# One change to a two-block transformer kernel: the low part of k in a tile of 128 rows per piece

## The chip, the cores and the metric

The kernel is one launch on one core of a Trainium2 chip. The metric is the device time of that launch in microseconds. TensorE multiplies matrices and writes to PSUM; in the profile its matmuls are PE and its loads of the stationary operand PEld. VectorE is DVE, ScalarE ACT, GpSimd POOL, and SyncE (SP) starts most transfers.

## The reference

One sequence of 1024 tokens with 1024 features goes through two layers of a first hybrid block and one layer of a second one. Each layer runs several branches on the normed input and mixes them. Two of the branches are softmax attention that reads the changed code:

- In each layer of the first block, a differential attention with a bias for each relative position. Each of 4 heads has two pieces m of q and k with 64 features; the two softmaxes are subtracted.
- In the second block, a causal attention whose logits get a decay, the difference of a running sum of log forget gates at the query and at the key. It has 4 heads of 64 features, and two heads lie in one projected block of 128 rows.

```python
logits = jnp.einsum('bqhmd,bkhmd->bhmqk', q_blk, k).astype(jnp.float32) * scale + bias
p = jax.nn.softmax(logits, axis=-1)
attn = p[:, :, 0] - lam * p[:, :, 1]
...
logits = jnp.einsum('bqhd,bkhd->bhqk', q[:, start:end], k[:, :end]) * scale
logits = logits + (f_q[..., :, None] - f_k[..., None, :])
```

Retention, pooling, a delta rule, a latent attention, a gated linear attention, gates and an MLP make up the rest; they are not touched.

## The kernel before

All products are in float32 accuracy from operands split in two parts: hi, the value rounded to the matmul's format, and lo, the rest. A product is hi x hi + hi x lo + lo x hi (`mm3`, lines L113 to L115), three matmuls into one PSUM bank. Most of the time goes into such dense products, with 128 rows of stationary operand and 256 or 512 columns.

**Logits of a piece.** A piece has 64 features, half of the array's 128 rows. `q_stack` puts hi and lo of a piece of q above each other in one page: rows [hi; lo] for m = 0 and [lo; hi] for m = 1. `k_stack` makes for each piece a page [hi; hi]. The first matmul (L386) then has 128 rows and gives q_hi k_hi + q_lo k_hi at once. What is missing is q_hi k_lo: `k_stack` keeps both pieces' lo parts in one page `kl`, that of m = 0 in rows 0 to 63 and that of m = 1 in rows 64 to 127, and the second matmul (L387) takes the 64 rows of its piece alone. Its stationary operand is the 64 rows of the q block that hold hi.

**First block, `attention_a`.** For each of 4 heads and 8 blocks of 128 queries, both pieces get logits of 1024 keys in two halves of 512: eight matmuls, L386 and L387 in turn. VectorE adds the bias and finds the maximum (L487), ScalarE takes the exponential (L491), VectorE inverts the sum (L492, L495), ScalarE scales the first piece (L496), VectorE subtracts the second (L497). Later TensorE transposes the result (L510), ScalarE and VectorE split it (L104, L105), and TensorE multiplies it with v. There are two banks for logits ("lg") and one for transposed blocks ("tp"). After each half of a head, a norm: sums on TensorE (L198), one small power on GpSimd (L141), and a broadcast of it on TensorE (L206).

**Second block, `fox`.** The same `k_stack`, `q_stack` and `qk_logits` feed `causal_heads`. Blocks reach only as far as the causal mask lets them, in parts of 512 or 256 keys. The last part of a block is followed by a matmul that adds the mask (L1461).

**What sets the order.** The projections of the next heads are put in a queue, and `pump` takes from it between the steps of attention. A scheduler then orders the instructions of each engine by priority when the kernel is built, and gives out pages. In the first block, all tiles of up to 512 columns come from 32 shared pages (tag "S"); a new tile waits until the last readers of the page's old tile are done. In the second block `q`, `kh` and `kl` have pages of their own.

Of the kernel before, what the change touches and what calls it, by code (L numbers as in the profile page):

```python
# [11 lines left out]
F32 = mybir.dt.float32  # L12
# [18 lines left out]
class Kern:  # L31
# [15 lines left out]
    # ---------------------------------------------------------------- tiles  # L47
# [4 lines left out]
    @contextmanager  # L52
    def phase(self, name):
        """A pool for the tiles of one phase; its bytes are waited for tile by tile."""
        old = self.pool
        with self.tc.tile_pool(name=self.nm(name), bufs=1, reuse_waits="tile") as self.pool:
            yield self.pool
        self.pool = old
# [38 lines left out]
    # ---------------------------------------------------------------- small helpers  # L97
# [19 lines left out]
    def log_sigmoid(self, out, x, n, tag):  # L117
        """out = log(sigmoid(x)) = min(x, 0) - log1p(exp(-|x|)), log1p(e) = 2 atanh(e / (2 + e))."""
        nc = self.nc
        if n <= 16:  # L120
            a, z, w = (self.small(n, tag + c, 2) for c in "azw")
        else:
            a, z, w = (self.T(tag + c, 1, F32, (P, n)) for c in "azw")
        nc.vector.scalar_tensor_tensor(out=a, in0=x, scalar=-1.0, in1=x, op0=ALU.mult, op1=ALU.max)
        nc.scalar.activation(a, a, AF.Exp, scale=-1.0)
        nc.vector.tensor_scalar_add(z, a, 2.0)
        nc.vector.reciprocal(z, z)
        nc.vector.tensor_tensor(out=z, in0=z, in1=a, op=ALU.mult)
        nc.vector.tensor_tensor(out=w, in0=z, in1=z, op=ALU.mult)
        nc.vector.tensor_scalar_mul(a, w, 1.0 / 13.0)  # L130
        for k in (11.0, 9.0, 7.0, 5.0, 3.0):
            nc.vector.scalar_tensor_tensor(out=a, in0=a, scalar=1.0 / k, in1=w, op0=ALU.add, op1=ALU.mult)
        nc.vector.scalar_tensor_tensor(out=a, in0=a, scalar=1.0, in1=z, op0=ALU.add, op1=ALU.mult)
        nc.vector.tensor_single_scalar(out=w, in_=x, scalar=0.0, op=ALU.min)
        nc.vector.scalar_tensor_tensor(out=out, in0=a, scalar=-2.0, in1=w, op0=ALU.mult, op1=ALU.add)

    def rsqrt_small(self, out, ss, n, mean):
        """out = (ss * mean + eps) ** -0.5 for a few columns."""
        nc = self.nc
        nc.vector.tensor_scalar(out=out, in0=ss, scalar1=mean, scalar2=EPS, op0=ALU.mult, op1=ALU.add)  # L140
        nc.gpsimd.tensor_tensor(out=out, in0=out, in1=self.mhalf[:, 0:n], op=ALU.pow)  # L141

    # ---------------------------------------------------------------- weights
    def wload(self, src, nk, n, hi=None, lo=None):
        """src: [128, nk, n] in DRAM -> accessors of the exact parts hi, lo of each k block."""
# [21 lines left out]
    def fm(self, out, w, X, half):  # L167
        """out[feature, token] += w^T X over all k blocks, for 512 tokens."""
        nk = len(w)
        for k in range(nk):  # L170
            xh, xl = X[k][half]
            self.mm3(out, w[k][0], w[k][1], xh, xl, k == 0, k == nk - 1)

    def tm(self, out, X, w, t):
        """out[token, feature] += X^T w for the 128 tokens of tile t."""
        nk = len(w)
        sl = slice((t % 4) * P, (t % 4 + 1) * P)
        for k in range(nk):
            xh, xl = X[k][t // 4]
            self.mm3(out, xh[:, sl], xl[:, sl], w[k][0], w[k][1], k == 0, k == nk - 1)  # L180

    # ---------------------------------------------------------------- norms
# [9 lines left out]
    def tok_sums(self, accs):  # L192
        """column sums of each [128, 512] page, token-major: [128, 4 per page] in PSUM."""
# [7 lines left out]
    def tok_bcast(self, r):  # L201
        """[128 tokens, n] -> [128, 128 n] in PSUM, the same in every partition."""
# [6 lines left out]
    def rnorm(self, acc, mean):  # L209
        """(mean * column sums of acc + eps) ** -0.5 in every partition, in PSUM."""  # L210
# [12 lines left out]
    # ---------------------------------------------------------------- set up  # L223
# [31 lines left out]
    def t5_table(self, rb, ohs):  # L255
        """bias of each relative position -1023..1023, each row shifted by one: skew[h][p][127 + j - p]."""
# [17 lines left out]
    # ---------------------------------------------------------------- first block  # L274
# [7 lines left out]
    def layer_consts(self, l, c, row, col):  # L282
# [21 lines left out]
        # retention decays; columns (direction, head)  # L304
# [30 lines left out]
    def silu_gate(self, ps, out):  # L335
        """out = (1 + tanh(x / 2)) * x = 2 silu(x), x in PSUM."""
# [4 lines left out]
    def q_stack(self, wq, X, half, nq=5):  # L341
        """Two 64-row pieces m of a 128-row block, scaled by 1/8: rows [hi; lo] (m = 0) or [lo; hi] (m = 1)."""
# [11 lines left out]
    def k_stack(self, wk, X, half, nk=5, nl=3):  # L354
        """Per piece rows [hi; hi], and lo at the rows where q has hi."""
# [4 lines left out]
        k0, k1, kl = self.T("kh", nk, F32R), self.T("kh", nk, F32R), self.T("kl", nl, F32R)  # L360
# [4 lines left out]
        nc.vector.tensor_tensor(out=kl[a], in0=pk[a], in1=k0[a].bitcast(F32), op=ALU.subtract)  # L365
        nc.vector.tensor_tensor(out=kl[b], in0=pk[b], in1=k1[b].bitcast(F32), op=ALU.subtract)  # L366
        return k0, k1, kl

    def qk_pack(self, qs, ks):
        return [[qs[0][m], qs[1][m]] for m in range(2)], [[ks[0][m], ks[1][m]] for m in range(2)], [ks[0][2], ks[1][2]]  # L370
# [8 lines left out]
    def qk_logits(self, out, QKK, m, qb, k0, kn, more=False):  # L379
        """out = q_m(block qb) . k_m(k0 : k0 + kn), all within one half."""  # L380
# [4 lines left out]
        rows = slice(m * 64, m * 64 + 64)  # L385
        mm(out, Q[m][qb // 4][:, sl], KH[m][half][:, o:o + kn], start=True, stop=False)  # L386
        mm(out, Q[m][qb // 4][rows, sl], KL[half][rows, o:o + kn], start=False, stop=not more)  # L387

    # -- the dense products of a layer, traced between the steps that wait for other engines
# [15 lines left out]
    def layer_dense(self, l, H, c, mixed, pre):  # L405
# [38 lines left out]
        # the first head: the work on the first half of the tokens goes ahead  # L444
# [20 lines left out]
    def attention_a(self, l, c, mixed):  # L465
        nc = self.nc
        tail = None
        for h in range(4):
# [6 lines left out]
            for qb in range(8):  # L475
# [4 lines left out]
                for m in range(2):  # L480
                    QKK = ({m: {half: qs[half][m]}}, {m: [ks[0][m], ks[1][m]]}, [ks[0][2], ks[1][2]])
# [57 lines left out]
    def diff_finish(self, h, half, osb, g, c, mixed):  # L539
        """in two steps; the first returns the second"""  # L540
# [234 lines left out]
    def out_proj(self, l, mixed, xold, xsave, sums, after):  # L775
        """x + mixed @ w_out, feature-major, one half of the tokens after the other."""
# [105 lines left out]
    def norm_next(self, half, xs, accs, wcol):  # L882
        """norm_half in steps"""
# [13 lines left out]
    def norm_between(self, half, xs, accs):  # L897
        """x2 = rmsnorm(x, final) -> DRAM; parts of rms_norm(x2, mix_pre).  mean(x2^2) = mean((x w)^2) r^2.  In steps."""
# [29 lines left out]
    # ---------------------------------------------------------------- second block  # L928
# [3 lines left out]
    def start_fills(self, H):  # L932
        """half 0 of the first units goes before half 1 of the tokens is there"""
# [6 lines left out]
    def fill(self, n=1):  # L940
        """The next n products of the gates, sigmoid(w_gate^T h + b) as 1 + tanh(./2), kept in DRAM until the branches are
        there: work for the tensor engine that nothing waits for."""
# [13 lines left out]
    def pre2(self, H):  # L956
        """the narrow projections: low-rank gate input (rows 0-15), b, a, f (rows 32-43), k_pe and its rotation (64-127)."""
# [83 lines left out]
    # ---- gated delta rule  # L1041
# [171 lines left out]
    def head_norm(self, t, o, gain, out):  # L1213
        """rms norm of each head's 64 columns of o: [128, 2, 2, 64] in PSUM, heads (b, m); out holds the gates.
        What waits for the norms is returned, to be traced later."""
# [21 lines left out]
    def delta_conv(self, b, j, H, cw):  # L1237
        """silu(causal convolution) of one 128-row block of q (j = 0), k, v; twice its value."""
# [99 lines left out]
    # ---- causal softmax attention, two heads of a block  # L1338
    def causal_heads(self, heads, steps):
        """Per head: start() -> logits(psum, qb, s, k0, kn, last), which adds q . k and the mask; V() -> [128, 4, 256] parts, columns vs;  # L1340
        out: [64 rows, 1024] feature-major pages.  A block's transposes follow the next block's logits."""
# [61 lines left out]
    def drain(self):  # L1403
        """traces what is left of the queue and forgets its results"""
        self.pump(len(self.dense))
        self.ready = {}
# [69 lines left out]
    def mla(self, H, out):  # L1476
# [4 lines left out]
        with self.phase("M") as mp:  # L1481
            # low-rank inputs, normed over their features
# [32 lines left out]
            def rope(ps, hs):  # L1515
                """rows 64-95 of ps rotated, at rows 64-95 of the result"""
# [86 lines left out]
    def gla_decays(self, g, up, gb):  # L1603
        """log decays, token-major [128, 4 of 8 tiles, 128 channels], kept in DRAM"""
# [12 lines left out]
    def gla(self, H, out):  # L1617
# [4 lines left out]
        with self.phase("G"):  # L1622
# [14 lines left out]
            # q, k, v  # L1637
# [108 lines left out]
    def merge(self, br):  # L1746
        """sum_i gate_i * (branch_i @ up_i), then @ w_out, feature-major; the last gates and the two halves of the tokens
        overlap."""
# [67 lines left out]
    def mlp(self, H, out):  # L1816
        """The first and the last part of the hidden layer take one half of the tokens after the other, so that the norms
        before and after have products beside them."""
# [42 lines left out]
        def finish(half, X):  # L1861
            """the last norm, in steps"""
# [116 lines left out]
def _lay(w, order):  # L1979
    """[K, N] -> [128, ...]: one run per partition for each group of columns, k blocks outermost."""  # L1980
# [67 lines left out]
def _cols(v):  # L2048
    """[..., n * 128] vectors -> [128, n] columns, one per block of 128."""
# [67 lines left out]
```

## Time and profile before

| | us |
|---|---|
| median of 3 runs | 3627.74 (3627.08 to 3628.82) |
| span of the profiled execution, first to last instruction | 3623.3 |
| what the median has beyond the span | 4.4 |
| TensorE matmuls busy | 3499.2 (97%) |
| VectorE, ScalarE, GpSimd busy | 1964.2, 1319.4, 89.6 |

The profiled execution's own time is not listed beside the runs; its span and the 4.4 us around it stand for it. The page counts the time from an instruction's start to its modelled end as busy. Matmuls are pipelined, so these times overlap: a matmul of 512 columns shows 0.39 us, but the next one may start 0.23 us after it. What TensorE really needs is read from starts. Idle time of the weight loader (PEld) is time in which no load ran; it costs something only where the matmul behind it is late.

### The profile page before, as it was taken

The page shows a single profiled execution, that of the slowest core. Times are in us where ns is not written, and L with a number is a line of the kernel's source. Part 1 is how long each engine was busy: PE and PEld are TensorE (multiplying, and loading weights), DVE is VectorE, ACT ScalarE, POOL GpSimd, SP SyncE. Part 2 cuts the span into 40 slices and gives each one's busy share as a digit, 9 for nine tenths or more (in the row PEclk, how much of TensorE's full clock was granted, in tenths as well). Part 3 has the DMA queues.
Part 4 walks back from the last instruction along what each step waited for, and adds up shares of the span by engine and source line. Part 5 has one row for each costly group of instructions (what it writes and reads, how often), then busy time and mean ns, then how long its engine had stood idle before and what let it go on. Part 6 is the DMA issues. An engine that isn't in the chain of part 4 may idle for free. (4 is left out here: it accounts for less than half of the span.)

```text
span 3623.3 us, 45361 instructions
## 1 busy us (share of the span) xinstructions
PE 3499.2 (97%) x18341; PEld 2835.2 (78%) x18341; DVE 1964.2 (54%) x3378; ACT 1319.4 (36%) x2098; POOL 89.6 (2%) x92
## 2 busy tenths in 40 slices
PE   7999999999999999999999999999999999999998
PEld 5777888777777788787777777877877778888886
DVE  6666654555666644556573466444268753333336
ACT  4555422233555422243322244454233442222222
POOL 0000000000000000000000000000000000000000
PEclk9999999999999999999999999999999999999999
DMA  5111111353110111354232211112156441111114
GB/s 182 47 40 41 42 48 51 112 183 110 49 41 30 31 33 57 108 161 153 74 119 62 81 47 57 47 53 87 53 191 227 143 126 49 53 47 47 53 55 149
DMA packets 138706, 302.34 MB, mean 83 GB/s; under 512 B 23944, under 2 KB 41336, under 8 KB 137984
## 3 DMA queue, kind: packets, MB, share of 16 engines
q1 hardware_dynamic: 129280, 282.65, 25.1%
q10 hardware_dynamic: 9216, 16.78, 1.2%
q8 instruction: 144, 2.36, 0.3%
q14 instruction: 66, 0.54, 0.0%
HBM read 245.30 MB, written 58.28 MB: 84 GB/s over the span
## 5 line engine op out<-in xcount | busy, mean ns | idle before, releaser
L113 PE MATMUL mm<-H,whi 128*128 128x512 f32 x2400 | 963.4, 402 | 28.1 <-DVE S L366 5.8
L115 PE MATMUL mm<-H,wlo 128*128 128x512 f32 x2400 | 952.0, 397 | 5.4 <-DVE wlo L105 5.4
L114 PE MATMUL mm<-H,whi 128*128 128x512 f32 x2400 | 951.7, 397 | 1.5 <-DVE H L105 1.5
L104 ACT CAST whi<-raw 128x1024 fp32r<-128x1024 f32 (+1 forms) x340 | 334.3, 984 | 857.0 <-PE mm L114 770.5
L105 DVE TENSOR_TENSOR wlo<-raw,whi 128x1024 fp32r<-128x1024 f32 (+1 forms) x340 | 387.4, 1141 | 440.5 <-ACT whi L104 427.8
L113 PEld LDWEIGHTS mm<-H,whi 128*128 128x128 f32 x2400 | 458.4, 191 | 133.5 <-issue 18.2
L115 PEld LDWEIGHTS mm<-H,wlo 128*128 128x128 f32 x2400 | 457.0, 190 | 103.5 <-DVE wlo L105 10.2
L114 PEld LDWEIGHTS mm<-H,whi 128*128 128x128 f32 x2400 | 457.3, 191 | 92.5 <-DVE H L105 2.6
L113 PE MATMUL mm<-whi,H 128*128 128x256 f32 x960 | 276.7, 289 | 3.5 <-DVE S L574 3.2
L114 PE MATMUL mm<-wlo,H 128*128 128x256 f32 x960 | 275.9, 288 | 1.4 <-DVE wlo L105 1.4
L115 PE MATMUL mm<-whi,H 128*128 128x256 f32 x960 | 274.4, 286 | 0.0
L113 PE MATMUL mm<-M,whi 128*128 128x512 f32 x640 | 249.8, 391 | 1.8 <-ACT whi L104 1.5
L115 PE MATMUL mm<-M,wlo 128*128 128x512 f32 x640 | 249.8, 391 | 0.2 <-DVE wlo L105 0.2
L114 PE MATMUL mm<-M,whi 128*128 128x512 f32 x640 | 249.8, 390 | 0.0
L113 PEld LDWEIGHTS mm<-whi,H 128*128 128x128 f32 x960 | 184.7, 193 | 8.6 <-issue 6.9
L114 PEld LDWEIGHTS mm<-wlo,H 128*128 128x128 f32 x960 | 184.8, 193 | 4.1 <-DVE wlo L105 2.0
L115 PEld LDWEIGHTS mm<-whi,H 128*128 128x128 f32 x960 | 184.8, 193 | 1.3 <-issue 1.2
L487 DVE CUSTOM_DVE_ANT_0 lg<-lg,strip 128x1024 f32<-128x1024 f32 x128 | 156.3, 1232 | 50.3 <-PE lg L387 49.6
L1853 DVE TENSOR_TENSOR Y<-Y,mm 128x512 f32<-128x512 f32 x112 | 77.0, 688 | 159.3 <-PE mm L115 159.2
L491 ACT ACTIVATE L<-lg,mx 128x1024 f32<-128x1024 f32 x128 | 142.5, 1119 | 29.0 <-DVE mx L487 15.6
L104 ACT CAST L<-tp 128x512 fp32r<-128x512 f32 x128 | 75.1, 586 | 207.1 <-PE tp L510 206.5
L113 PEld LDWEIGHTS mm<-M,whi 128*128 128x128 f32 x640 | 120.2, 188 | 28.1 <-ACT whi L104 2.0
(450 smaller groups left out, 5082.6 us busy)
## 6 DMA issues: line engine op xcount, KB each, us to landing
raw<-in_w_in SPq DMA_DIRECT2D x106, 512.0 KB, 3.7
raw<-in_w_out SPq DMA_DIRECT2D x48, 512.0 KB, 4.1
raw<-in_w_gate SPq DMA_DIRECT2D x46, 512.0 KB, 3.7
raw<-in_w_mlp_in SPq DMA_DIRECT2D x40, 512.0 KB, 3.6
raw<-in_w_mlp_out SPq DMA_DIRECT2D x40, 512.0 KB, 3.6
Y<-gates SPq DMA_DIRECT2D x64, 256.0 KB, 5.0
gates<-gs ACTq DMA_DIRECT2D x60, 256.0 KB, 2.0
mix<-S SPq DMA_DIRECT2D x48, 256.0 KB, 2.1
```

The source lines that it names most:

```text
L104: nc.scalar.copy(hi, src)
L105: nc.vector.tensor_tensor(out=lo, in0=src, in1=hi.bitcast(F32), op=ALU.subtract)
L113: mm(out, lh, rh, start=start, stop=False)
L114: mm(out, lh, rl, start=False, stop=False)
L115: mm(out, ll, rh, start=False, stop=stop)
L487: nc.vector.tensor_tensor_reduce(out=lg, in0=lg, in1=strip[:, w0:w0 + 1024], op0=ALU.add, op1=ALU.min, scale=-1.0, scalar=3.0e38, accum_ou ...
L491: nc.scalar.activation(pm, lg, AF.Exp, bias=mx, scale=-1.0, accum_out=sm)
L1853: nc.vector.tensor_tensor(out=Y[d][half], in0=Y[d][half], in1=pt, op=ALU.add)
```

## The change

`k_stack` gets two tiles for the lo parts instead of one. Tile `l0` holds the lo part of piece 0 in rows 0 to 63 and zeros in rows 64 to 127; `l1` holds zeros in rows 0 to 63 and the lo part of piece 1 in rows 64 to 127. The zeros are written by GpSimd, one memset for each tile at each call. The second matmul of the logits then takes all 128 rows of the q block, and its rows of q_lo meet zeros. Callers pass the tile of the piece. In the second block the tag `kl` has five pages instead of three. The rest of the diff takes out comments and docstrings.

```diff
-    def k_stack(self, wk, X, half, nk=5, nl=3):
-        """Per piece rows [hi; hi], and lo at the rows where q has hi."""
+    def k_stack(self, wk, X, half, nk=5, nl=5):
+
         nc = self.nc
         a, b = slice(0, 64), slice(64, 128)
         pk = self.ps("mm")
         self.fm(pk, wk, X, half)
-        k0, k1, kl = self.T("kh", nk, F32R), self.T("kh", nk, F32R), self.T("kl", nl, F32R)
+        k0, k1 = self.T("kh", nk, F32R), self.T("kh", nk, F32R)
+        l0, l1 = self.T("kl", nl, F32R), self.T("kl", nl, F32R)
+        nc.gpsimd.memset(l0[b].bitcast(F32), 0.0)
+        nc.gpsimd.memset(l1[a].bitcast(F32), 0.0)
         nc.scalar.copy(k0[a], pk[a])
         nc.scalar.copy(k0[b], pk[a])
         nc.scalar.copy(k1[b], pk[b])
         nc.scalar.copy(k1[a], pk[b])
-        nc.vector.tensor_tensor(out=kl[a], in0=pk[a], in1=k0[a].bitcast(F32), op=ALU.subtract)
-        nc.vector.tensor_tensor(out=kl[b], in0=pk[b], in1=k1[b].bitcast(F32), op=ALU.subtract)
-        return k0, k1, kl
+        nc.vector.tensor_tensor(out=l0[a], in0=pk[a], in1=k0[a].bitcast(F32), op=ALU.subtract)
+        nc.vector.tensor_tensor(out=l1[b], in0=pk[b], in1=k1[b].bitcast(F32), op=ALU.subtract)
+        return k0, k1, l0, l1
...
-        rows = slice(m * 64, m * 64 + 64)
         mm(out, Q[m][qb // 4][:, sl], KH[m][half][:, o:o + kn], start=True, stop=False)
-        mm(out, Q[m][qb // 4][rows, sl], KL[half][rows, o:o + kn], start=False, stop=not more)
+        mm(out, Q[m][qb // 4][:, sl], KL[m][half][:, o:o + kn], start=False, stop=not more)
...
-                    QKK = ({m: {half: qs[half][m]}}, {m: [ks[0][m], ks[1][m]]}, [ks[0][2], ks[1][2]])
+                    QKK = ({m: {half: qs[half][m]}}, {m: [ks[0][m], ks[1][m]]}, {m: [ks[0][2 + m], ks[1][2 + m]]})
```

The lines of the logits become L388 and L389 and most lines behind them move by two. The scheduler leaves nearly all instructions of TensorE, VectorE and ScalarE where they were. On TensorE, a block of logits of the second head stands so before (lg is the bank, S are pages: first k, then q):

```order
L510 MATMUL tp_1423<-c_ident,L_1263 128x128 x4
L386 MATMUL lg_1439<-S_1044,S_1226 128x512
L387 MATMUL lg_1439<-S_1046,S_1226 128x512
L386 MATMUL lg_1439<-S_1117,S_1226 128x512
L387 MATMUL lg_1439<-S_1119,S_1226 128x512
L386 MATMUL lg_1450<-S_1045,S_1227 128x512
L387 MATMUL lg_1450<-S_1046,S_1227 128x512
L386 MATMUL lg_1450<-S_1118,S_1227 128x512
L387 MATMUL lg_1450<-S_1119,S_1227 128x512
L510 MATMUL tp_1430<-c_ident,L_1263 128x128 x4
```

The same place on TensorE now:

```order
L512 MATMUL tp_1435<-c_ident,L_1275 128x128 x4
L388 MATMUL lg_1451<-S_1050,S_1238 128x512
L389 MATMUL lg_1451<-S_1052,S_1238 128x512
L388 MATMUL lg_1451<-S_1126,S_1238 128x512
L389 MATMUL lg_1451<-S_1128,S_1238 128x512
L388 MATMUL lg_1462<-S_1051,S_1239 128x512
L389 MATMUL lg_1462<-S_1053,S_1239 128x512
L388 MATMUL lg_1462<-S_1127,S_1239 128x512
L389 MATMUL lg_1462<-S_1129,S_1239 128x512
L512 MATMUL tp_1442<-c_ident,L_1275 128x128 x4
```

The places are the same. The two pieces read S_1046 both before; now piece 0 reads S_1052 and piece 1 S_1053.

GpSimd's queue from the norm of the first layer's input to the norms of the first and second head stands so before (rn is the small power of a norm):

```order
L141 TENSOR_TENSOR rn_336<-rn_336,mhalf 128x4
L141 TENSOR_TENSOR rn_1248<-rn_1248,mhalf 128x4
L141 TENSOR_TENSOR rn_1617<-rn_1617,mhalf 128x4
L141 TENSOR_TENSOR rn_1987<-rn_1987,mhalf 128x4
L141 TENSOR_TENSOR rn_2422<-rn_2422,mhalf 128x4
```

The same stretch of that queue now, up to the second of these norms of heads:

```order
L141 TENSOR_TENSOR rn_339<-rn_339,mhalf 128x4
L362 MEMSET S_659 64x512
L363 MEMSET S_660 64x512
L362 MEMSET S_1052 64x512
L363 MEMSET S_1053 64x512
L362 MEMSET S_1128 64x512
L363 MEMSET S_1129 64x512
L141 TENSOR_TENSOR rn_1260<-rn_1260,mhalf 128x4
L362 MEMSET S_1606 64x512
L363 MEMSET S_1607 64x512
L362 MEMSET S_1692 64x512
L363 MEMSET S_1693 64x512
```

Six memsets stand in front of the first head's first norm and four in front of its second; four more stand in front of the fifth norm of a layer, and the same again in the second layer. S_1606 and S_1607, for the third head, wait for the last logits that read the first head's k.

On ScalarE, between two blocks of the second head, the order before was (L104 with whi is the hi part of a weight load, L348 and L349 are q's copies, L104 with tp a split of transposed blocks):

```order
L496 ACTIVATE L_1263<-L_1263,smx_1264 128x1024
L348 ACTIVATE S_1306<-mm_1281 64x512
L349 ACTIVATE S_1307<-mm_1281 64x512
L104 CAST L_1166<-tp_1312 128x4x128
L104 CAST whi_1563<-raw_1561 128x1024
L104 CAST L_1167<-tp_1319 128x4x128
```

And at the same place on ScalarE now:

```order
L498 ACTIVATE L_1275<-L_1275,smx_1276 128x1024
L104 CAST whi_1575<-raw_1573 128x1024
L104 CAST L_1178<-tp_1324 128x4x128
L348 ACTIVATE S_1318<-mm_1293 64x512
L349 ACTIVATE S_1319<-mm_1293 64x512
L104 CAST L_1179<-tp_1331 128x4x128
```

The weight's hi part and one split have moved in front of q's two copies. Exchanges of this size stand at a few places in each layer of the first block; in the second block only the memsets are new.

## Rows read from the trace of the kernel before

**Rows 1.** The page's part 1: busy us, share of the span, instructions of each engine.

```profile
PE 3499.2 (97%) x18341; PEld 2835.2 (78%) x18341; DVE 1964.2 (54%) x3378; ACT 1319.4 (36%) x2098; POOL 89.6 (2%) x92
```

**Rows 2.** Windows: stretch, length, then busy us of PE, PEld, DVE, ACT, POOL; clock, DMA.

```profile
82.00:437.00 355.00, 354.19 (x1914) 271.41 (x1913) 234.07 (x416) 192.23 (x300) 7.05 (x7) 1.00 0.13 40
...
2312.00:2505.00 193.00, 188.91 (x1021) 148.20 (x1020) 90.37 (x187) 99.76 (x185) 0.00 (x0) 0.96 0.19 57
```

**Rows 3.** Timeline, 307 to 311 us: start, duration, engine, line, operation [idle before].

```profile
307.55 0.39 PE L113 MATMUL mm<-H,whi 128*128 128x512 f32 x1
307.55 0.19 PEld L114 LDWEIGHTS mm<-H,whi 128*128 128x128 f32 x1
307.78 0.39 PE L114 MATMUL mm<-H,whi 128*128 128x512 f32 x1
...
309.68 0.18 PEld L387 LDWEIGHTS lg<-S,S 64*128 64x128 f32 x1 [0.24 <-issue]
309.68 0.50 PE L387 MATMUL lg<-S,S 64*128 64x512 f32 x1
...
310.11 0.50 PE L386 MATMUL lg<-S,S 128*128 128x512 f32 x1
...
310.54 0.49 PE L387 MATMUL lg<-S,S 64*128 64x512 f32 x1
```

**Rows 4.** Lines L386 (first row) and L387: idle of loads; counts, ns min/median/max.

```profile
  issue: 42.4, 172
...
L387 PE MATMUL lg<-S,S x256: 490/498/792, 54.4 to 1258.9; 64*128 64x512 f32 x128
...
L387 PE MATMUL lg<-kl,q x64: 378/381/579, 2312.0 to 2504.9; 64*128 64x256 f32 x48, 64*128 64x512 f32 x16
...
  issue: 67.1, 271
```

**Rows 5.** Timeline in retention, 525 us.

```profile
525.78 0.30 PEld L673 LDWEIGHTS lg<-S 64*128 64x128 f32 x4 [0.17 <-issue]
```

**Rows 6.** Timeline of TensorE in the decay attention, 2424 to 2434 us.

```profile
2424.52 0.36 PE L386 MATMUL lg<-kh,q 128*128 128x256 f32 x1
2424.82 0.38 PE L387 MATMUL lg<-kl,q 64*128 64x256 f32 x1
2425.13 0.28 PE L1461 MATMUL lg<-mskb,identb 128*128 128x256 bf16 x1
...
2433.02 0.28 PE L115 MATMUL pv<-pt,v 128*64 128x256 f32 x1
2433.14 0.28 PE L113 MATMUL pv<-pt,v 128*64 128x256 f32 x1
```

**Rows 7.** Timeline of TensorE behind a group of logits, 205 us.

```profile
205.73 0.50 PE L113 MATMUL mm<-H,whi 128*128 128x512 f32 x1
206.07 0.40 PE L114 MATMUL mm<-H,whi 128*128 128x512 f32 x1
```

**Rows 8.** Timeline, VectorE's last step and the transposition behind it, 212 to 215 us.

```profile
212.76 1.28 DVE L497 SCALAR_TENSOR_TENSOR L<-L,smx,L 128x1024 f32<-128x1024 f32 x1
...
214.66 0.60 PE L510 MATMUL tp<-c_ident,L 128*128 128x128 f32 x4
```

**Rows 9.** Waits, 100 to 430 us: who waited <- for whom: us, times, longest.

```profile
DVE L L105 <- ACT L L104: 17.4, 21, 1.6
DVE smx L492 <- ACT L L491: 17.3, 29, 1.3
DVE L L497 <- ACT L L496: 14.5, 19, 1.2
```

**Rows 10.** Timeline of GpSimd, a memset in the second block.

```profile
1829.21 1.80 POOL L1107 MEMSET BT<- 128x2048 f32 x1
```

**Rows 11.** Timeline, a norm of the first head, 200 to 202 us.

```profile
200.09 1.01 POOL L141 TENSOR_TENSOR rn<-rn,mhalf 128x4 f32<-128x4 f32 x1 [46.13 <-DVE smx L492]
...
201.41 0.97 PEld L206 LDWEIGHTS pv<-c_ident,rn 128*128 128x128 f32 x8
```

More of the change, by code (lines that the diff above doesn't have):

```diff
@@ L364, in k_stack @@
         nc.scalar.copy(k1[a], pk[b])
-        nc.vector.tensor_tensor(out=kl[a], in0=pk[a], in1=k0[a].bitcast(F32), op=ALU.subtract)
-        nc.vector.tensor_tensor(out=kl[b], in0=pk[b], in1=k1[b].bitcast(F32), op=ALU.subtract)
-        return k0, k1, kl
+        nc.vector.tensor_tensor(out=l0[a], in0=pk[a], in1=k0[a].bitcast(F32), op=ALU.subtract)
+        nc.vector.tensor_tensor(out=l1[b], in0=pk[b], in1=k1[b].bitcast(F32), op=ALU.subtract)
+        return k0, k1, l0, l1
     def qk_pack(self, qs, ks):
-        return [[qs[0][m], qs[1][m]] for m in range(2)], [[ks[0][m], ks[1][m]] for m in range(2)], [ks[0][2], ks[1][2]]
+        return [[qs[0][m], qs[1][m]] for m in range(2)], [[ks[0][m], ks[1][m]] for m in range(2)], [[ks[0][2 + m], ks[1][2 + m]] for m in range(2)]
     def qk_stacks(self, wq, wk, X):
```

## The prediction, as it was made before the changed kernel ran

> **What bounds the kernel now.** I read the busy times first. TensorE is busy 3499.2 of 3623.3 us, 97%; the other engines have far less [rows 1]. A busy matmul row is no proof of work at full rate, so I then cut out, by windows, the three stretches in which the changed logits are made: the attention of the first block in its first layer (54 to 437 us), the same in its second layer (868 to 1259), and the decay attention of the second block (2312 to 2505). From 82 to 437 us TensorE is busy 354.2 of 355 at a granted clock of 1.00, VectorE 234.1, ScalarE 192.2; in the decay attention TensorE has 188.9 of 193 at 0.96 of full speed, VectorE 90.4, ScalarE 99.8 [rows 2]. The second layer reads like the first. TensorE's own stream of instructions sets the length of these stretches, so what one matmul takes from its start to the next start counts one for one, unless another engine then falls behind.
>
> Third, the timeline. In a dense product, matmuls of 512 columns on 128 rows start 0.23 us apart (307.55, 307.78): the weight load of the second starts with the matmul before it, and its 0.19 us lie beside that matmul. In the logits the starts are 0.43 apart (309.68, 310.11, 310.54). The load of L387, 64 rows, starts only together with its own matmul, after the loader idled 0.24 us for "issue", that is for nothing that the profile shows [rows 3]. The view of each line says that this is the rule and that the load of the L386 behind it, 128 rows again, suffers too: loads of L387 idle on "issue" 271 times of 320, 67.1 us, those of L386 172 times of 320, 42.4 us, 0.25 each [rows 4]. Retention's L673, of 64 rows behind a transposition of 128, has such an idle as well [rows 5]. So it is the change of the row count, on the way into a 64-row matmul and on the way out, and not this line.
>
> **The change, part by part.** (a) The second matmul of a pair had 64 rows and gets 128, with the same columns and the same q. The counts [rows 4]: 256 of L387 in the first block, all of 512 columns (4 heads, 8 blocks, 2 pieces, 2 halves, 2 layers), and 64 in the decay attention, 48 of them of 256 columns and 16 of 512. With their L386 that is 272 pairs of 512 and 48 of 256. At 512 columns each of the two changes makes a start 0.43 after the one before instead of 0.23: 2 x 272 x 0.20 = 109 us. At 256 columns the starts are 0.30 and 0.31 apart (2424.52, 2424.82, 2425.13), against 0.12 in the 128-row stream at 2433.02: 2 x 48 x 0.19 = 18 us [rows 6]. Some 20 of the 640 changes stand beside a transposition or a 256-column product of another kind, where I read about 0.10: 2 us off, and 1 for rounding. 124 us.
>
> (b) The tail of the way out. Where a dense product follows the last L387, its first matmul is late by the 0.20 just counted, and the second still by 0.1: L113 at 205.73, L114 at 206.07, 0.34 where 0.23 is normal [rows 7]. About 80 groups of logits end so (the 32 of the decay attention end in the mask): 80 x 0.1 = 8 us. Together 132 us of TensorE's stream.
>
> (c) What comes back as waits. TensorE reaches the transpositions (L510) sooner, and these need the probabilities that VectorE finishes with L497. One distance: L497 ends at 214.04, L510 starts at 214.66, 0.6 us later [rows 8]. The eight matmuls of a block save 1.6 us in all, so in some blocks L510 will wait, unless VectorE's input, the logits, comes sooner by as much. VectorE's reserve: from 82 to 437 us it is busy 234.1 us [rows 2], and waits for ScalarE that no faster TensorE shortens are 17.4 + 17.3 + 14.5 = 49 us [rows 9]; 283 us, in a stretch that becomes 355 - 120 pairs x 0.40 = 307. TensorE stays the last, by 24 us. The loss is nothing at the lower end; the upper end is half of the gain, 66 us, which would need VectorE's waits not to shrink at all. I take a value near the lower end, to which the reserve is nearer: 0.3 us in a third of the 128 blocks, 12 us, the decay attention included.
>
> (d) Forty memsets of 64 rows x 512 on GpSimd, two for each of 20 calls. The one row of a memset of size, 2048 columns, took 1.80 us [rows 10]; by columns some 0.5 each, 20 us on an engine that is busy 2% [rows 1]. No matmul needs a cleared tile before the logits of that head. What they can hold up is the power of L141 behind them on the same queue, and its cover is thin: it ends at 201.10, and the loads of L206 that need it start at 201.41 [rows 11]. In the new order they stand in front of 6 of the 16 norms of heads, up to six in a row; but what they wait for, a free page, is older than the norm's input. I cost this at 0; at two us for each of the six it would be 12.
>
> (e) Pages. Each half of a k projection holds four of the 32 shared pages and not three, two more for a head. The order moves by some places around the second to fourth head and the end of attention, and the logits stand where they stood. 0, within plus or minus 5. The two subtractions on VectorE stay as they are, into two tiles.
>
> Sum: 124 + 8 - 12 = 120 us. The span is 3623.3; the runs have 3627.74 in the median, 4.4 more, which lies around the span and stays. 3503.3 + 4.4 = 3508 us, 3.3% less.
>
> Against this speaks a rule of the Trainium skill, "TensorE: Matmul & The Clock Gate", Part 3, The mechanism: a weight load overlaps a running matmul only where their row groups differ. By it two 128-row loads in a row would never overlap, each logits matmul would still pay its load and its stream, and the sum would be near 0. The trace does not agree: at 307.55 a load of 128 rows runs beside a matmul of 128 rows [rows 3].
>
> **The rivals.** First, VectorE takes over: the gain of the attention stretches ends in front of L510. For it: the 0.6 us, and VectorE at 76% of the new stretch (234 of 307). Against it: the reserve of 24 us. With half of the gain lost the time is 3628 - 66 = 3562. Chance 0.06.
>
> Second, the pair does not overlap after all, because two loads of the same block of q, into one bank, are held up by something else than the row count. For it: no pair of that kind, both of 128 rows, stands in the trace. Against it: dense products add into one bank too, and overlap. Time 3628, within 5. Chance 0.03, the rule above included.
>
> Third, on the other side: GpSimd's queue. A memset waits for the last readers of its page, for two heads in each layer matmuls of the head before, and the power of L141 stands behind it; TensorE then stands at L206. That is slower than before once each of the six places costs more than 132 / 6 = 22 us. A norm comes every 47 us (46.1 idle and 1.0 [rows 11]); at half of that, 23.6 us, it is 142 - 132 = 10 us slower, 3638. Against it: those matmuls must be done before the norm's own input is there. Chance 0.02.
>
> **How the numbers follow.** Forecast 0.89, the rivals 0.11. The forecast's own range: without loss 3628 - 132 = 3496, and 2 us for TensorE waits that go along; with three times my loss, 36, and the 12 of (d), 3628 - 132 + 48 = 3544. So 3494 to 3544; the first rival at its half lies outside it. What a measurement of this kernel can tell from no change is 0.2%, 7 us. Faster by more: the forecast and the first rival, 0.95. Within: the second, 0.03. Slower: 0.02.
>
> **What would show it.** Starts in a pair of logits 0.23 apart at 512 columns and 0.12 at 256; the loads of both lines 0.19 us and beside the matmul before, their idle on "issue" down from 110 us to under 15. From the first to the last logits of the first layer about 330 us and not 383, of the decay attention about 170 and not 193. New waits of TensorE for L497 and for the exponential, some 10 us. Memsets of about 0.5 us on GpSimd, and L141 no later behind its input. I am wrong if the pair stays at 0.43, or if it falls to 0.23 and waits of more than 40 us stand in front of L510, the logits or L206.

## The result and the profile after

The changed kernel took 3524.11 us in the median (3517.07 to 3526.03, four runs) against 3627.41 (3623.29 to 3628.82, four runs) before: ratio 0.9705, 95% interval 0.969 to 0.9719. 103 us are gone where 120 were forecast; the forecast of 3508 is 16 us too low, and the time lies in its range. The profiled execution took 3525.61 us, with a span of 3523.8 at a mean granted clock of 0.981; before, the span was 3623.3 at 0.982.

The page's part 1, as in [rows 1]:

```profile
PE 3389.1 (96%) x18341; PEld 2829.7 (80%) x18341; DVE 1953.0 (55%) x3378; ACT 1319.5 (37%) x2098; POOL 110.3 (3%) x132
```

Matmuls, weight loads and VectorE's work are the same in number; GpSimd has its 40 memsets more, and 20.7 us. TensorE still bounds the kernel.

The timeline of the changed kernel at a block of logits behind a group of transpositions, and at its end, as in [rows 3] and [rows 7]:

```profile
280.81 0.60 PE L512 MATMUL tp<-c_ident,L 128*128 128x128 f32 x4
281.14 0.19 PEld L388 LDWEIGHTS lg<-S,S 128*128 128x128 f32 x1
281.17 0.48 PE L388 MATMUL lg<-S,S 128*128 128x512 f32 x1
281.25 0.19 PEld L389 LDWEIGHTS lg<-S,S 128*128 128x128 f32 x1
281.48 0.40 PE L389 MATMUL lg<-S,S 128*128 128x512 f32 x1
281.48 0.19 PEld L388 LDWEIGHTS lg<-S,S 128*128 128x128 f32 x1
281.71 0.40 PE L388 MATMUL lg<-S,S 128*128 128x512 f32 x1
281.72 0.19 PEld L389 LDWEIGHTS lg<-S,S 128*128 128x128 f32 x1
...
282.88 0.39 PE L389 MATMUL lg<-S,S 128*128 128x512 f32 x1
...
283.10 0.40 PE L113 MATMUL mm<-H,whi 128*128 128x512 f32 x1
...
283.34 0.39 PE L114 MATMUL mm<-H,whi 128*128 128x512 f32 x1
```

Read the starts. From the second matmul of the block on they are 0.23 to 0.24 apart, where [rows 3] had 0.43, and each load now starts with the matmul before it. The way out costs nothing more: L113 starts 0.22 after the last L389 and L114 0.24 after L113; in [rows 7] it was 0.34. One distance stays longer than 0.23: the first L388 behind the transpositions needs 0.31 (281.17 to 281.48). The load for L389 starts 0.08 us after the matmul before it, at 281.25, and not with it; L389 then follows its load by 0.23 as everywhere.

Each line's view of the loads, L388 first and then L389: what they idled for, as in [rows 4]:

```profile
  issue: 1.1, 1
...
  issue: 0.4, 2
```

42.4 and 67.1 us have become 1.1 and 0.4. TensorE in the decay attention, as in [rows 6]:

```profile
2345.04 0.28 PE L389 MATMUL lg<-kl,q 128*128 128x256 f32 x1
2345.16 0.29 PE L388 MATMUL lg<-kh,q 128*128 128x256 f32 x1
2345.28 0.28 PE L389 MATMUL lg<-kl,q 128*128 128x256 f32 x1
2345.40 0.28 PE L1463 MATMUL lg<-mskb,identb 128*128 128x256 bf16 x1
```

At 256 columns the starts are 0.12 apart and were 0.30. Windows from the first to the last L389 of the three stretches, and of the stretch between the second and the third, which the change does not touch; columns as in [rows 2], the last but two the granted clock:

```profile
53.50:392.80 339.30, 334.58 (x2072) 293.52 (x2071) 241.71 (x439) 204.60 (x321) 11.73 (x16) 0.99 0.15 50
824.30:1169.80 345.50, 340.94 (x2093) 296.75 (x2092) 238.11 (x429) 200.87 (x315) 11.21 (x15) 0.99 0.15 48
1169.80:2232.90 1063.10, 1018.69 (x5689) 839.17 (x5687) 586.78 (x1098) 346.23 (x586) 46.87 (x44) 0.97 0.26 84
2232.90:2405.70 172.80, 165.08 (x1022) 140.30 (x1020) 86.66 (x185) 99.83 (x185) 1.55 (x3) 0.99 0.20 62
```

The same four of the kernel before:

```profile
54.40:437.20 382.80, 380.26 (x2061) 294.06 (x2060) 250.35 (x449) 204.53 (x321) 7.05 (x7) 0.99 0.14 45
868.30:1258.90 390.60, 388.90 (x2082) 299.44 (x2081) 245.57 (x435) 200.90 (x315) 7.05 (x7) 0.98 0.14 42
1258.90:2312.00 1053.10, 1009.96 (x5699) 832.20 (x5698) 582.27 (x1088) 346.52 (x586) 44.29 (x39) 0.98 0.28 85
2312.00:2504.90 192.90, 188.81 (x1021) 148.10 (x1020) 90.37 (x187) 99.76 (x185) 0.00 (x0) 0.96 0.19 57
```

The three attention stretches are 43.5, 45.1 and 20.1 us shorter, together 108.7. The untouched stretch is 10.0 longer, at a lower granted clock, though it has ten matmuls fewer: the new order lets them run in the stretches before it. The rest of the span moves by about 1 us, and 99.5 remain.

Where the 108.7 us come from can be counted. For each matmul in the three stretches I took the distance to the next start and subtracted what its columns need in a stream of 128 rows (0.227 us at 512 columns, 0.120 at 256, 0.112 below). The sums of this excess, in us; what ran at half clock, 1.2 GHz, stands apart:

| where the excess lies | before | after |
|---|---|---|
| between the matmuls of a block's logits | 96.0 | 9.7 |
| from the last of them to the next product | 22.8 | 1.8 |
| from that product to the one behind it | 6.1 | -1.0 |
| waits, each over 0.35 | 10.7 | 19.4 |
| small delays elsewhere | 0.8 | 8.8 |
| into the logits, and third product behind them | -3.1 | -4.7 |
| at half clock | 16.8 | 4.9 |
| sum | 150.1 | 38.9 |

The sums differ by 111.2. The three stretches are 108.7 shorter because 23 more matmuls, most of them of 256 columns, now stand in them (11, 11 and 1 by the counts above), and these need the other 2.5 us.

The waits that came. Waits of TensorE and of its weight loader (PEld) from 54 to 1260 us of the changed kernel (who waited <- for whom: us, times, longest):

```profile
PE pv L206 <- POOL rn L141: 4.2, 7, 0.9
PE mm L114 <- DVE wlo L105: 3.1, 4, 1.1
...
PE tp L512 <- DVE L L105: 0.9, 2, 0.7
...
PEld tp L512 <- DVE L L105: 5.0, 14, 0.9
```

The first two before, and the one that then stood longest in front of the transpositions, under the old line numbers:

```profile
PE pv L206 <- POOL rn L141: 1.6, 2, 0.8
PE mm L114 <- DVE wlo L105: 1.4, 2, 1.1
...
PEld tp L510 <- DVE mx L487: 1.9, 8, 0.2
```

They are spread: norms' broadcasts, split weights, and, in front of the transpositions (L512), VectorE's split of an earlier transposed block (L105). No row of TensorE names L499, the subtraction that was L497 before. VectorE's own waits from 100 to 390 us, as in [rows 9]:

```profile
DVE L L499 <- ACT L L498: 15.6, 21, 1.2
DVE lg L489 <- PE lg L389: 12.2, 5, 3.7
DVE smx L494 <- ACT L L493: 11.7, 18, 1.3
...
DVE L L105 <- ACT L L104: 5.6, 10, 2.5
```

The three waits for ScalarE sum to 32.9 us and were 49, in a stretch that was longer. VectorE still waits 12.2 us for the logits, so it does not take over as the bound.

GpSimd's timeline, a norm's power with memsets behind it, and an earlier norm's input on VectorE, as in [rows 10] and [rows 11]:

```profile
183.88 0.16 DVE L140 TENSOR_SCALAR rn<-tp 128x4 f32<-128x4 f32 x1 [1.14 <-PE tp L198]
184.19 1.01 POOL L141 TENSOR_TENSOR rn<-rn,mhalf 128x4 f32<-128x4 f32 x1 [33.59 <-DVE smx L494]
...
266.05 1.01 POOL L141 TENSOR_TENSOR rn<-rn,mhalf 128x4 f32<-128x4 f32 x1 [36.22 <-DVE smx L494]
267.12 0.52 POOL L362 MEMSET S<- 64x512 f32 x1
267.70 0.52 POOL L363 MEMSET S<- 64x512 f32 x1
```

A memset takes 0.52 us, and L141 starts 0.15 us after its input is there (183.88 + 0.16 to 184.19).

### The profile page after: what moved, and what is told of

The parts are those of the page before. It is cut to its first block, busy times and chain, and to the rows that moved or that the text cites. A ratio compares the mean times of both kernels' runs of the same rounds, so it can differ in the third digit from the quotient of the medians.

```text
span 3523.8 us, 45480 instructions
## 1 busy us (share of the span) xinstructions
PE 3389.1 (96%) x18341; PEld 2829.7 (80%) x18341; DVE 1953.0 (55%) x3378; ACT 1319.5 (37%) x2098; POOL 110.3 (3%) x132
## 5 line engine op out<-in xcount | busy, mean ns | idle before, releaser
L113 PE MATMUL mm<-H,whi 128*128 128x512 f32 x2400 | 961.0, 401 | 28.6 <-DVE S L369 5.0
L114 PE MATMUL mm<-H,whi 128*128 128x512 f32 x2400 | 951.9, 397 | 1.6 <-DVE H L105 1.6
L104 ACT CAST whi<-raw 128x1024 fp32r<-128x1024 f32 (+1 forms) x340 | 334.4, 984 | 869.2 <-PE mm L114 774.9
L105 DVE TENSOR_TENSOR wlo<-raw,whi 128x1024 fp32r<-128x1024 f32 (+1 forms) x340 | 387.3, 1140 | 435.4 <-ACT whi L104 423.2
L113 PEld LDWEIGHTS mm<-H,whi 128*128 128x128 f32 x2400 | 458.3, 191 | 128.6 <-ACT H L107 7.2
L114 PEld LDWEIGHTS mm<-H,whi 128*128 128x128 f32 x2400 | 458.0, 191 | 93.3 <-DVE H L105 2.6
L113 PE MATMUL mm<-whi,H 128*128 128x256 f32 x960 | 276.7, 289 | 3.9 <-DVE S L576 3.2
L114 PE MATMUL mm<-wlo,H 128*128 128x256 f32 x960 | 275.0, 287 | 3.1 <-DVE wlo L105 3.1
L113 PE MATMUL mm<-M,whi 128*128 128x512 f32 x640 | 249.6, 391 | 1.8 <-ACT whi L104 1.6
L114 PE MATMUL mm<-M,whi 128*128 128x512 f32 x640 | 249.8, 390 | 0.0
L113 PEld LDWEIGHTS mm<-whi,H 128*128 128x128 f32 x960 | 184.8, 193 | 6.5 <-issue 4.0
L114 PEld LDWEIGHTS mm<-wlo,H 128*128 128x128 f32 x960 | 185.0, 193 | 5.1 <-DVE wlo L105 4.2
L113 PEld LDWEIGHTS mm<-M,whi 128*128 128x128 f32 x640 | 120.3, 188 | 28.1 <-ACT whi L104 2.0
L115 PEld LDWEIGHTS mm<-M,wlo 128*128 128x128 f32 x640 | 120.6, 188 | 25.7 <-DVE wlo L105 0.6
```

Of the source, the lines that this page charges most:

```text
L104: nc.scalar.copy(hi, src)
L105: nc.vector.tensor_tensor(out=lo, in0=src, in1=hi.bitcast(F32), op=ALU.subtract)
L113: mm(out, lh, rh, start=start, stop=False)
L114: mm(out, lh, rl, start=False, stop=False)
L115: mm(out, ll, rh, start=False, stop=stop)
```

## The experiments

The theory: each change of the row count costs TensorE 0.2 us, nothing else in the change has a price, and the stretch that grew did so by the clock. The rivals: the price belongs to the 64-row matmul itself; the memsets or pages took part of the forecast gain; VectorE or GpSimd holds TensorE up. The first four experiments ran on one chip, where the kernel before took 3632.28 us (3628.48 to 3637.24, 13 runs), the last three on another, at 3627.38 (3619.56 to 3639.93, 7 runs).

**The changed kernel again**, with no edit.

> The changed kernel once more, unedited. Its first four runs took 3517 to 3526 us, ratio 0.9705. In its profiled run the work between the first layer's attention of layer two and the decay attention, whose instructions are the same as before, is 10.0 us longer, and there 64.7 us stand at half clock instead of 34.2. Theory (clock): these stretches of half clock fall differently from run to run; expected are times from 3515 to 3527, median 3523, and in a profile a stretch at half clock of another length between the same instructions, the stretch longer or shorter by a third of a microsecond or more for each. Rival (a real cost of the change, for instance of the pages): the stretch between the second layer's attention and the decay attention takes 1063 us again, with the same 65 us at half clock.

Measured: 3519.63 us (3515.02 to 3523.18), ratio 0.9688 (0.9674 to 0.9703). The three attention stretches repeat within 0.3 us (339.2, 345.2, 173.1). The untouched stretch, in this profile, in that of the 96-row kernel below, whose instructions there are the same, and in that of the kernel with grouped logits below, which is the kernel before in this stretch:

```profile
1170.70:2230.30 1059.60, 1016.82 (x5688) 837.66 (x5688) 586.68 (x1098) 346.03 (x586) 46.87 (x44) 0.97 0.27 84
```

```profile
1171.50:2227.10 1055.60, 1011.25 (x5689) 834.41 (x5687) 586.61 (x1098) 346.11 (x586) 46.93 (x44) 0.98 0.27 85
```

```profile
1211.70:2274.80 1063.10, 1018.86 (x5699) 838.77 (x5697) 583.12 (x1088) 346.45 (x586) 44.30 (x39) 0.97 0.27 84
```

Its time at half clock, added up from the record of the granted clock, is 34.3 us before (1053.1 us long), 44.4 in the 96-row kernel (1055.6), 58.0 here (1059.6) and 64.9 in the first profile (1063.1): about a third of a microsecond for each, as expected. The grouped kernel has none of the change and the matmuls of before in this stretch; it has 61.4 us at half clock there and 1063.1 us. So the 10 us are no cost of the change; the first profile of the kernel before lies at the lower end of what this stretch does.

**All of the change but the row count:**

```diff
-        mm(out, Q[m][qb // 4][:, sl], KL[m][half][:, o:o + kn], start=False, stop=not more)
+        rows = slice(m * 64, m * 64 + 64)
+        mm(out, Q[m][qb // 4][rows, sl], KL[m][half][rows, o:o + kn], start=False, stop=not more)
```

> All of the change stays (two tiles for the low parts, the memsets, five pages), only the second matmul takes the piece's 64 rows as before. Theory (all of the gain is the row count): 3627 us, within 5; pairs of logits start 0.43 us apart at 512 columns again, and the loads of the second matmul idle on issue in most cases. Rival (memsets and pages cost some of the 120 us forecast, which is why 104 were measured): 3635 to 3645. Rival (the tile per piece itself gives something, for instance by later reuse of a page): under 3615.

Measured: 3634.97 us (3627.53 to 3644.94, ten runs), ratio 1.0004 (0.9995 to 1.0014). On this chip that is the kernel before, within -2 and +5 us; the 3627 expected was the first measurement's time of the kernel before, which takes 5 us more on this chip. Its line view of the second matmul's loads:

```profile
  issue: 66.8, 272
```

All of the 67.1 us of [rows 4] are back, with the tiles, memsets and pages of the change in place, and by the count of starts above the first two rows of the table come to 119 us again, as before the change. Tiles, memsets and pages cost at most 5 us; the gain is the row count.

**The kernel before, first block's logits grouped by row count:**

```diff
                     for kh in range(2):
-                        self.qk_logits(lg[:, kh * 512:kh * 512 + 512], QKK, m, qb, kh * 512, 512)
+                        nc.tensor.matmul(lg[:, kh * 512:kh * 512 + 512], QKK[0][m][half][:, sq], QKK[1][m][kh], start=True, stop=False)
+                    for kh in range(2):
+                        nc.tensor.matmul(lg[:, kh * 512:kh * 512 + 512], QKK[0][m][half][rows, sq], QKK[2][kh][rows], start=False, stop=True)
```

> The kernel before, but in the attention of the first block the four matmuls of a piece are issued as 128, 128, 64, 64 rows in place of 128, 64, 128, 64; the same 64-row matmuls, half as many changes of the row count. Theory (each change of the row count costs 0.20 us, the 64-row matmul itself nothing): 128 groups lose two changes each, 128 x 2 x 0.20 = 51 us; 3576 us, within 8; second of two 64-row matmuls 0.23 us after the first. Rival (a load for fewer rows than the array has always waits, whatever stands ahead of it): 3627 us, starts 0.43 apart between the two 64-row matmuls too.

Measured: 3586.15 us (3581.77 to 3592.76), ratio 0.9874 (0.9859 to 0.9888): 46 us gained, 41 to 51 by the interval, with as many 64-row matmuls as before. The rival is out. In its profile, counted from starts as above, the first two rows of the table are 44 us lower, for the 51 expected, and the excess at half clock about 7 lower, so part of the 46 may be the clock's. The time lies 10 us above the 3576 expected, half of it because the kernel before takes 5 us more on this chip. One detail of my expectation failed. The timeline of TensorE at a block (x2: two in a row, with the time of both):

```profile
89.88 0.61 PE L485 MATMUL lg<-S,S 128*128 128x512 f32 x2
90.43 0.73 PE L487 MATMUL lg<-S,S 64*128 64x512 f32 x2
91.08 0.73 PE L485 MATMUL lg<-S,S 128*128 128x512 f32 x2
91.75 0.73 PE L487 MATMUL lg<-S,S 64*128 64x512 f32 x2
```

Two 64-row matmuls take 0.65 us (90.43 to 91.08), not 0.43 + 0.23. Over all blocks the medians are 0.33 into the 64 rows, 0.34 between the two, 0.32 out and 0.32 between the next two. My reading is that a change in this order costs 0.1 at its place and 0.1 on the next matmul, and that where the count changes at every matmul both fall on one start, 0.43. By the medians the sum is as expected: four starts take 1.30 us here and 1.71 before, 0.41 less for two changes.

**96 rows instead of 128 in the second matmul of every first piece:**

```diff
-        mm(out, Q[m][qb // 4][:, sl], KL[m][half][:, o:o + kn], start=False, stop=not more)
+        rows = slice(0, 128 if m else 96)
+        mm(out, Q[m][qb // 4][rows, sl], KL[m][half][rows, o:o + kn], start=False, stop=not more)
```

> The changed kernel, with 96 rows instead of 128 in the second matmul of every first piece (rows 0 to 95: 64 of low part and 32 of zeros); half of the 320 pairs. Theory (what costs is a change between classes of height: up to 64 rows, and more than 64): nothing, 3524 us, within 5; in the trace of before the few 96-row matmuls start 0.23 us after a 128-row one. Rival (any difference of row counts costs 0.20 us in and 0.20 out): 136 pairs of 512 columns x 0.40 and 24 of 256 x 0.38 = 64 us more, 3588 us.

Measured: 3524.39 us (3519.74 to 3530.15), ratio 0.9703 (0.9688 to 0.9717); its interval overlaps with that of the changed kernel on this chip, and the 64 us of the rival are excluded. Loads of the second matmul, by shape (count, busy us, mean ns, idle):

```profile
L390 PEld LDWEIGHTS lg<-S,S 96*128 96x128 f32 x128 | 24.6, 192 | 3.1 <-issue 0.3
L390 PEld LDWEIGHTS lg<-S,S 128*128 128x128 f32 x128 | 24.4, 190 | 4.7 <-issue 0.2
```

A load of 96 rows next to 128 does not wait; one of 64 does. The Trainium skill, "TensorEngine Tiling (Array Packing)", Key Properties, says that changing the tiling mode drains TensorE; the same page lists, under Available Configurations, modes of 128, 64 and 32 rows. The 0.2 us for a change between 128 and 64 rows and the nothing for 96 agree with that, if 96 rows run in the mode of 128; no run shows what TensorE does in the 0.2 us.

**The change in the first block alone**, the decay attention as before (the old helper is kept beside the new one):

```diff
-                    self.push(("fk", b, half), lambda b=b, half=half: self.k_stack(W(("foxk", b), 128), H, half))
+                    self.push(("fk", b, half), lambda b=b, half=half: self.k_stack_old(W(("foxk", b), 128), H, half))
...
-                    self.qk_logits(o, QKK, mh, qb, k0, kn, last)
+                    self.qk_logits(o, QKK, mh, qb, k0, kn, last, slice(mh * 64, mh * 64 + 64))
```

> The change in the first block's attention alone; the decay attention of the second block keeps the shared tile and the 64-row matmul. Theory (gains add, by place): from first to last logits of the decay attention 193 us again instead of 173, 3544 us, within 5; starts 0.30 us apart at 256 columns. Rival (VectorE or ScalarE limits the decay attention, and part of its 20 us came from elsewhere): a stretch of 180 us or less, under 3532 us.

Measured: 3535.60 us (3531.14 to 3540.18), ratio 0.9742 (0.9716 to 0.9768). That is 12 us above the two kernels below, which ran beside it, and not 20: a partial miss. The window of its decay attention:

```profile
2225.30:2415.90 190.60, 187.09 (x1020) 146.73 (x1019) 90.43 (x187) 99.69 (x185) 0.00 (x0) 0.97 0.19 58
```

The stretch itself gives 17.8 us (190.6 against 172.8 of the first profile and 172.9 of the next kernel), some 2 of them by 6.8 us less at half clock, so the gain belongs to this place. The profiled runs of this kernel and of the next are 15.4 us apart (3537.01 and 3521.63); with ratios each uncertain by 0.25%, 9 us, the medians do not tell 12 from 18.

**Each memset four times:**

```diff
-        nc.gpsimd.memset(l0[b].bitcast(F32), 0.0)
-        nc.gpsimd.memset(l1[a].bitcast(F32), 0.0)
+        for _ in range(4):
+            nc.gpsimd.memset(l0[b].bitcast(F32), 0.0)
+            nc.gpsimd.memset(l1[a].bitcast(F32), 0.0)
```

> The changed kernel with each of its 40 memsets on GpSimd issued four times: 120 more of 0.52 us, 62 us more on GpSimd. Theory (the memsets are covered): the time of the changed kernel, 3523 us, within 4. Rival (GpSimd's queue delays the power of L141, and TensorE with it, at 6 of the 16 norms of a head): up to 6 x 3.1 us = 19 us more for six further memsets in front of each, 3542 us.

Measured: 3523.62 us (3521.42 to 3526.3), ratio 0.9711 (0.969 to 0.9731): no cost that could be measured, and the 19 us of the rival are excluded. The unedited changed kernel did not run on this chip, so the finer comparison is that of the profiles: the three attention stretches take 339.2, 345.5 and 172.9 us, against 339.3, 345.5 and 172.8. TensorE's wait for the norm's power, from 54 to 1260 us:

```profile
PE pv L206 <- POOL rn L141: 4.2, 7, 0.9
```

It is the same row as with single memsets, so GpSimd's queue is not what it waits for.

**The memsets on VectorE:**

```diff
-        nc.gpsimd.memset(l0[b].bitcast(F32), 0.0)
-        nc.gpsimd.memset(l1[a].bitcast(F32), 0.0)
+        nc.vector.memset(l0[b].bitcast(F32), 0.0)
+        nc.vector.memset(l1[a].bitcast(F32), 0.0)
```

> The changed kernel with the 40 memsets on VectorE instead of GpSimd. Theory (VectorE has a reserve of some 25 us in each layer's attention, and a memset there takes no more than the 0.52 us on GpSimd): the same within 5, 3519 to 3528 us. Rival (VectorE is nearly the bound, or its memset stands waiting for a free page in front of work that TensorE waits for): 10 us or more above, 3534 us and up, with idle of VectorE in front of the memsets and new waits of TensorE for VectorE.

Measured: 3523.93 us (3517.07 to 3527.82), ratio 0.9709 (0.9686 to 0.9733): the same. VectorE's line view of one of the two memsets:

```profile
L362 DVE MEMSET S<- x16: 485/485/485, 33.0 to 1059.7; 64x512 f32 x16
```

0.49 us each, 20 us in all on VectorE, with nothing lost; its L206 wait is again 4.2 us in 7 times. In the first layer's attention VectorE is busy 248.2 us instead of 241.7, so it has a reserve of at least some 6 us there; the whole reserve that the prediction reckoned was not put to the test. None of the variants beats the changed kernel.

## Why the prediction was right, and where it was off

The mechanism held: TensorE's starts set the three stretches, the change of the row count was the cost, and it went. By its steps:

(a) The second matmul, 124 us. The price was right: before, 631 of the 640 changes of the row count stand in the trace without a wait beside them, with an excess of 121.6 us, half clock included; that is 123 for 640. What failed is that all of it would go. Afterwards 9.7 us remain between the logits' matmuls and 1.8 behind them. 253 L388 of 512 columns have an L389 behind them at 0.258 us in the mean, with a median of 0.235: the first pair behind a transposition had 0.41 and still has 0.31, because its weight load starts late (281.25, 0.08 us behind the matmul before it). Some 50 pairs stand behind a transposition, and some 40 more behind other products, most of them at 0.31 too; the prediction had some 20 such cases and took 2 us off. At full clock the two rows of the table fall by 107 us.

(b) The tail of the way out, 8 us: from 6.1 to -1.0, 7.1 us. Right.

(c) Waits that come back, 12 us: waits over 0.35 us grew by 8.7 and the small delays by 8.0, 17 in all. The size was near, but not the place: the prediction had L510 wait for L497, and no row shows that wait. Some 3 of the 17 us stand in front of L512, where the rows name L105. The rest is spread over norms, products with freshly split weights, logits and dense products; why those inputs come no sooner was not traced. The reserve of 24 us was also reckoned from waits for ScalarE that were taken as fixed, 49 us, and these fell to 32.9.

(d), (e) The memsets and the pages, 0 within their bounds: the row-count experiment leaves at most 5 us for both, and four times the memsets, or the memsets on VectorE, change nothing that could be measured.

The 4.4 us around the span were too much: the profiled execution of the changed kernel took 1.8 us more than its span (3525.61 and 3523.8), and runs of the kernel before on the first experiments' chip 2.2 (3635.5 and 3633.3). So most likely the profiled execution of the kernel before was itself some 2 us faster than the median.

What the sum did not have is the clock. In the three stretches the half-clock time fell from 35.7 to 10.9 us and its excess by 11.9; in the untouched stretch it rose from 34.3 to 64.9, for 10.0 us. In the profile the two nearly cancel. Together the attention gave 108.7 where 120 were forecast, and that is closer than the steps were. At full clock the table falls by 99 us, some 21 less than forecast: (a) is 17 short and (c) 5. The clock gave 12 back that were not in the sum, which was luck. The 103 us of the first measurement and the 113 of the repetition (0.9688) lie on both sides of the 108.7.

The rule that the prediction argued against, of the Trainium skill, "TensorE: Matmul & The Clock Gate", Part 3, The mechanism, would have left the time at 3628. As that list states it, it is contradicted here: at 281.72 the load of L389, 128 rows, starts with the matmul of L388, 128 rows, for the same bank, and such matmuls start 0.23 to 0.24 apart. The paragraph above that list lets a load also run ahead when it goes to a background weight buffer; no run shows whether that is what happens here. The three rivals fall with the 339.3, 345.5 and 172.8 us of the stretches, the rows of L389, and the memset experiments.

## What to carry to other kernels

Where TensorE is the bound, read starts, not durations, and look at the loader's idle "on issue": matmuls of 64 rows among ones of 128 cost 0.2 us for each change of the row count, and filling the other rows with zeros, written by an idle engine, takes that away. Where the rows can't be filled, put matmuls of equal row count side by side; that gave 46 us in the first block alone, without any new tile, where the whole change gave 113 on the same chip. Ask of every saving what stood behind the saved delay: here a lead that the loader had lost at each transposition was hidden by the row change and came to light without it.

## What the runs showed of the hardware beside this

- A change between 128 and 64 rows costs 0.2 us; one between 128 and 96 rows nothing that could be measured (in the median 0.236 us from a 96-row matmul of 512 columns to the next, 0.230 from a 128-row one).
- In the three attention stretches the time at half clock was 35.7 us with the 64-row matmul and 47.5 in the kernel with only the row count put back; it was 6.8 to 10.9 us in the five profiles with 128 or 96 rows. The two mixed kernels lie between: 20.9 with grouped logits, 13.7 with the change in the first block alone. Taken by place, the decay attention has 10.2 to 13.9 us in the four profiles with 64 rows there and 0 to 3.4 in the other five; the first block's two stretches have 21.9 and 37.3 us with 128 and 64 rows in turn, 7.0 with grouped logits, and 3.5 to 7.6 with 128 or 96 rows. So in these profiles the time at half clock goes with the changes of the row count; by what mechanism was not tried.
- Profiles of the same instructions differ by 10 us in one stretch of 1050 us (1053.1 before and 1063.1 in the grouped kernel), with 34.3 and 61.4 us at half clock, and the runs of one kernel by 20 us (3619.56 at a mean clock of 0.985, 3639.93 at 0.978).
